# Binary cross entropy on one core: the stores of the full chunks go from the GpSimd queue to the SyncE queue

## The chip, the cores and the metric

The kernel runs on one core of a Trainium2 chip. The metric is the device time of one execution in microseconds; of several runs the median is taken. The core has five engines with instruction streams of their own. Here DVE (VectorE) and ACT (ScalarE) compute, and POOL (GpSimd), SP (SyncE) and, once, ACT issue transfers between the chip's memory (HBM) and the on-chip memory (SBUF). The transfers themselves run on 16 DMA engines, which all of these queues share.

## The reference

```
pred, target: 8192 x 8192, float32; target is 0 or 1
pred = clip(pred, 1e-7, 1 - 1e-7)
return -(target * log(pred) + (1 - target) * log(1 - pred))
```

Since a target is 0 or 1, the kernel computes -log|p + t - 1|, which is -log(p) for t = 1 and -log(1 - p) for t = 0.

## The kernel before

The arrays are taken as flat runs of elements and cut into 39 chunks. Each chunk lies over all 128 partitions: 8192 columns for chunk 0, 14336 for chunks 1 to 35, and 6656, 6656 and 1024 for the last three, called a, b and c (chunks 36 to 38). In the code z is 35, the last full chunk.

The pred values of a chunk are loaded into one of three slots of `ring_p` (slot k mod 3; a, b and c share the slot of chunk 33), are worked on in place, and are stored from there. So load_p(k+2) writes the slot of chunk k-1 and may not begin before store(k-1) has landed. The targets go to `ring_t`, one buffer of a single chunk's width, and are cast to bf16 on the way; so load_t(k+1) may not begin before both halves of merge(k) have read the old targets.

The work on a chunk is done in two halves (whole for a, b and c):

- clip (L85, DVE): the two bounds, in one instruction;
- merge (L91, DVE): p + (t - 1); then Abs (L94, ACT) and Ln (L95, ACT);
- negate (L99, DVE): times -1.

The order on each engine is that of the program, written out by hand under `manual_schedule`. Each round of the main loop (L110 to L120) issues: both merges of chunk k; load_t(k+1); both negates of k; both clips of k+1; store(k); load_p(k+2). An engine that waits holds up all that is behind it in its own stream, and no other engine.

All loads go through POOL's queue, but for load_p(0), which ACT issues. The function `store` (L75) chooses the queue of a store: POOL for chunks 0 to 35, SP for a, b and c. In POOL's stream a round is therefore load_t(k+1), store(k), load_p(k+2). The last round issues no load_p. After the loop come the loads of a, b and c, and then negate, clip and merge of the tail with the stores between them (L121 to L141). The store of the last chunk is cut into 108, 12 and 8 partitions.

Of the kernel before, what the change touches and what calls it, by code (L numbers as in the profile page):

```python
# [1 line left out]

# [4 lines left out]

EPS = 1e-7

WIDE = 14336  # L10
SLOTS = 3
TAIL = (6656, 6656, 1024)
ROWS = (108, 12, 8)


@with_exitstack
def kernel(
    ctx: ExitStack,
    tc: tile.TileContext,
    pred: bass.AP,  # L20
    target: bass.AP,
    out: bass.AP,
):
    nc = tc.nc
    fp32 = mybir.dt.float32
    low = mybir.dt.bfloat16
    Alu = mybir.AluOpType
    Act = mybir.ActivationFunctionType
    P = nc.NUM_PARTITIONS

    R, C = pred.shape
    total = R * C // P
    rest = total - sum(TAIL)
    n = rest // WIDE
    first = rest - n * WIDE
    assert 0 < first <= WIDE and n > 4 and sum(TAIL) <= WIDE
    spots = [(first, 0)]
    spots += [(WIDE, k % SLOTS * WIDE) for k in range(1, n + 1)]
    c = (n + 1) % SLOTS * WIDE
    for w in TAIL:  # L40
        spots.append((w, c))
        c += w
    n = len(spots)
    z = n - 1 - len(TAIL)
    starts = [sum(w for w, _ in spots[:k]) * P for k in range(n)]

    pool = ctx.enter_context(tc.tile_pool(name="rings", bufs=1))
    ring_p = pool.tile([P, SLOTS * WIDE], fp32, name="ring_p", tag="ring_p")
    ring_t = pool.tile([P, WIDE], low, name="ring_t", tag="ring_t")
    warm = pool.tile([1, 8], fp32, name="warm", tag="warm")  # L50

    def chunk(ap, k):
        flat = ap.rearrange("r c -> (r c)")
        w = spots[k][0]
        return flat[starts[k] : starts[k] + w * P].rearrange("(p w) -> p w", p=P)

    def cols(ring, k, part, c):
        w = spots[k][0]
        i, m = part
        return ring[:, c + i * w // m : c + (i + 1) * w // m]  # L60

    def p_of(k, part=(0, 1)):
        return cols(ring_p, k, part, spots[k][1])

    def t_of(k, part=(0, 1)):
        return cols(ring_t, k, part, spots[k][1] % WIDE)

    def load_p(k):
        queue = nc.scalar if k == 0 else nc.gpsimd
        queue.dma_start(out=p_of(k), in_=chunk(pred, k))  # L70

    def load_t(k):
        nc.gpsimd.dma_start(out=t_of(k), in_=chunk(target, k))  # L73

    def store(k):  # L75
        queue = nc.sync if k > z else nc.gpsimd
        r = 0
        for rows in ROWS if k == n - 1 else (P,):
            queue.dma_start(out=chunk(out, k)[r : r + rows, :], in_=p_of(k)[r : r + rows, :])  # L79
            r += rows  # L80
        assert r == P

    def clip(k, *part):
        p = p_of(k, *part)
        nc.vector.tensor_scalar(  # L85
            out=p, in0=p, scalar1=EPS, scalar2=1 - EPS, op0=Alu.max, op1=Alu.min
        )

    def merge(k, *part):
        p, t = p_of(k, *part), t_of(k, *part)  # L90
        nc.vector.scalar_tensor_tensor(  # L91
            out=p, in0=t, scalar=1.0, in1=p, op0=Alu.subtract, op1=Alu.add
        )
        nc.scalar.activation(out=p, in_=p, func=Act.Abs)  # L94
        nc.scalar.activation(out=p, in_=p, func=Act.Ln)  # L95

    def negate(k, *part):
        p = p_of(k, *part)
        nc.vector.tensor_scalar(out=p, in0=p, scalar1=-1.0, scalar2=None, op0=Alu.mult)  # L99

    halves = (0, 2), (1, 2)
    with tc.manual_schedule():
        load_p(0)
        load_t(0)
        load_p(1)
        nc.vector.memset(warm, 1.0)  # L106
        nc.scalar.activation(out=warm, in_=warm, func=Act.Ln)  # L107
        for h in halves:
            clip(0, h)
        for k in range(z):  # L110
            for h in halves:
                merge(k, h)
            load_t(k + 1)
            for h in halves:
                negate(k, h)
            for h in halves:
                clip(k + 1, h)
            store(k)
            if k + 2 <= z:
                load_p(k + 2)  # L120
        for h in halves:  # L121
            merge(z, h)
        a, b, c = range(z + 1, n)
        for j in a, b, c:
            load_p(j)
            load_t(j)
        negate(z, halves[0])
        clip(a)
        negate(z, halves[1])
        store(z)  # L130
        merge(a)
        clip(b)
        merge(b)
        negate(a)
        store(a)
        clip(c)
        merge(c)
        negate(b)
        store(b)
        negate(c)  # L140
        store(c)  # L141


# [1 line left out]
_INS = ['pred', 'target']  # L145
_OUTS = [((8192, 8192), 'float32')]


# [23 lines left out]
```

## Time and profile before

| what | value |
|---|---|
| median of 3 runs | 1867.39 us (1866.88 to 1868.22) |
| the profiled execution | 1868.84 us |
| its span | 1867.1 us |
| DVE busy | 1118.2 us (60%) |
| ACT busy | 901.7 us (48%) |
| POOL busy | 283.3 us (15%) |
| POOL's queue (q0) | 16272 packets, 659.56 MB, 98.5% of 16 engines |
| SP's queue (q1) | 448 packets, 7.34 MB, 0.9% |
| ACT's queue (q10) | 144 packets, 4.19 MB, 0.6% |
| full chunks: issue to landing, median | pred 44.3 us, store 31.0 us, target 35.2 us |

How the views are read. The summary cuts the span into 40 slices and gives the busy share of each in tenths; the DMA row is the mean over the 16 DMA engines, and the row of GB/s counts the bytes that land, so that a target load counts half of what it reads. The waits say who waited for whom, with the total, the number of waits and the longest. The chain goes back from the last instruction through what released each step; "issue" is time in which the engine of the chain waited for nothing that the profile shows. In a timeline a line has the start, the duration, the engine, the line of the kernel and the operation, and in brackets how long the engine was idle before and what ended that. A line of a window has the stretch and its length, the busy time of DVE, ACT and POOL with the number of instructions, the granted clock of TensorE, the DMA share and GB/s; a transfer's packet is booked where it starts, so that very short windows can show a share over 1.

### The profile page before, as it was taken

To read this page: it belongs to the slowest core of one execution; us is meant where nothing else is said; L and a number is where in the kernel's file an instruction comes from. 1 tells how busy PE (TensorE), PEld (TensorE's weight loads), DVE (VectorE), ACT (ScalarE), POOL (GpSimd) and SP (SyncE) were. 2 spreads that over 40 slices of the span, in tenths; PEclk is the share of its full clock that TensorE was granted. 3 is DMA by queue.
4 is the path that set the end of the run, shared out by engine and by line. 5 is a ranking of instruction groups with operands and counts; after the bars stand their busy time and mean duration, and the time that the engine had idled before them with its cause. 6 is when DMAs were issued, how large, how long until landed. Compare 5 with 4: busy or idle time off the path is not lost.

```text
span 1867.1 us, 695 instructions
## 1 busy us (share of the span) xinstructions
DVE 1118.2 (60%) x226; ACT 901.7 (48%) x152; POOL 283.3 (15%) x117
## 2 busy tenths in 40 slices
DVE  4675665655556555665665556655566665556664
ACT  3555444444555555444444555555544444455555
POOL 0121111111111101111111111101111111111100
DMA  9999999999999999999999999999999999999998
GB/s 331 336 373 373 364 355 359 356 355 355 354 354 359 373 373 373 370 356 362 356 354 358 354 354 356 367 373 373 373 362 360 359 354 359 354 354 354 360 366 346
DMA packets 16869, 671.14 MB, mean 359 GB/s; under 512 B 1888, under 2 KB 1888, under 8 KB 2272
## 3 DMA queue, kind: packets, MB, share of 16 engines
q0 software_dynamic: 16272, 659.56, 98.5%
q1 hardware_dynamic: 448, 7.34, 0.9%
q10 hardware_dynamic: 144, 4.19, 0.6%
q14 instruction: 5, 0.04, 0.0%
HBM read 536.87 MB, written 268.44 MB: 431 GB/s over the span
## 4 chain that ended last, share of the span: by engine, by line
DMA 67%; issue 28%; DVE 2%; ACT 2%; POOL 0%; POOLq 0%; DVEq 0%; PEldq 0%
DMA ring_t<-in_target_dram 67%; DVE ring_p L91 2%; ACT ring_p L95 1%; ACT ring_p L94 1%; DVE ring_p L99 0%; POOL out_dram L79 0%; POOL ring_p L70 0%; DVEq L167 0%; POOLq L73 0%; POOLq L79 0%; DVEq L91 0%; PEldq L167 0%
## 5 line engine op out<-in xcount | busy, mean ns | idle before, releaser
L94 ACT ACTIVATE ring_p<-ring_p 128x7168 f32<-128x7168 f32 (+3 forms) x75 | 451.6, 6021 | 943.5 <-DVE ring_p L91 943.5
L91 DVE SCALAR_TENSOR_TENSOR ring_p<-ring_t,ring_p 128x7168 f32<-128x7168 bf16 (+3 forms) x75 | 554.8, 7436 | 236.9 <-DMA ring_t<-in_target_dram 236.8
L99 DVE TENSOR_SCALAR ring_p<-ring_p 128x7168 f32<-128x7168 f32 (+3 forms) x75 | 285.0, 3801 | 475.0 <-ACT ring_p L95 475.0
L95 ACT ACTIVATE ring_p<-ring_p 128x7168 f32<-128x7168 f32 (+3 forms) x75 | 452.1, 6028 | 2.4
L85 DVE TENSOR_SCALAR ring_p<-ring_p 128x7168 f32<-128x7168 f32 (+3 forms) x75 | 281.8, 3798 | 20.1 <-DMA ring_p<-in_pred_dram 20.1
L79 POOL DMA_DIRECT2D out_dram<-ring_p x36 | 127.4, 3540 | 730.3 <-DVE ring_p L99 730.3
L73 POOL DMA_DIRECT2D ring_t<-in_target_dram x39 | 20.7, 532 | 802.9 <-DVE ring_p L91 802.1
L70 POOL DMA_DIRECT2D ring_p<-in_pred_dram x38 | 135.3, 3560 | 0.0
L107 ACT ACT_TABLE_LOAD x1 | 1.3, 1283 | 1.1 <-PEq L156 1.1
L106 DVE MEMSET warm<- 1x8 f32 x1 | 0.1, 65 | 0.8 <-PEq L156 0.8
L107 ACT ACTIVATE warm<-warm 1x8 f32<-1x8 f32 x1 | 0.2, 208 | 0.0
L156 POOL MEMSET const-float32-0.0<- 128x1 f32 x1 | 0.1, 98 | 0.2 <-issue 0.2
L156 POOL MEMSET const-bfloat16-1.0<- 128x1 bf16 x1 | 0.1, 101 | 0.0
L156 POOL MEMSET const-float32-1.0<- 128x1 f32 x1 | 0.1, 98 | 0.0
L156 POOL MEMSET const-uint8-127<- 128x1 uint8 x1 | 0.1, 98 | 0.0
## 6 DMA issues: line engine op xcount, KB each, us to landing
ring_p<-in_pred_dram POOLq DMA_DIRECT2D x35, 7168.0 KB, 44.3
out_dram<-ring_p POOLq DMA_DIRECT2D x35, 7168.0 KB, 31.0
ring_t<-in_target_dram POOLq DMA_DIRECT2D x35, 3584.0 KB, 35.2
ring_p<-in_pred_dram POOLq DMA_DIRECT2D x2, 3328.0 KB, 33.6
out_dram<-ring_p SPq DMA_DIRECT2D x2, 3328.0 KB, 15.1
ring_p<-in_pred_dram ACTq DMA_DIRECT2D x1, 4096.0 KB, 19.5
out_dram<-ring_p POOLq DMA_DIRECT2D x1, 4096.0 KB, 21.4
ring_t<-in_target_dram POOLq DMA_DIRECT2D x2, 1664.0 KB, 28.8
```

Of the source, the lines that this page charges most:

```text
L70: queue.dma_start(out=p_of(k), in_=chunk(pred, k))
L73: nc.gpsimd.dma_start(out=t_of(k), in_=chunk(target, k))
L79: queue.dma_start(out=chunk(out, k)[r : r + rows, :], in_=p_of(k)[r : r + rows, :])
L85: nc.vector.tensor_scalar(out=p, in0=p, scalar1=EPS, scalar2=1 - EPS, op0=Alu.max, op1=Alu.min)
L91: nc.vector.scalar_tensor_tensor(out=p, in0=t, scalar=1.0, in1=p, op0=Alu.subtract, op1=Alu.add)
L94: nc.scalar.activation(out=p, in_=p, func=Act.Abs)
L95: nc.scalar.activation(out=p, in_=p, func=Act.Ln)
L99: nc.vector.tensor_scalar(out=p, in0=p, scalar1=-1.0, scalar2=None, op0=Alu.mult)
L106: nc.vector.memset(warm, 1.0)
L107: nc.scalar.activation(out=warm, in_=warm, func=Act.Ln)
L156: nc = _bacc.Bacc("TRN2", target_bir_lowering=False, num_devices=1)
```

## The change

One line of `store` chooses another queue. The stores of chunks 0 to 34 are issued by SP instead of POOL, as those of a, b and c are already. The store of chunk 35 stays on POOL, behind the loads of the tail. POOL's stream in a round is then load_t(k+1), load_p(k+2), and SP's is store(k). What each transfer depends on is unchanged: a store waits for its negate, and a load of pred for the store that frees its slot.

```diff
     def store(k):
-        queue = nc.sync if k > z else nc.gpsimd
+        queue = nc.gpsimd if k == z else nc.sync
         r = 0
         for rows in ROWS if k == n - 1 else (P,):
             queue.dma_start(out=chunk(out, k)[r : r + rows, :], in_=p_of(k)[r : r + rows, :])
```

## The prediction

> **What bounds the kernel now.** I read the summary of the span first, then the waits, the chain, one period of the timeline, and last short windows at the beginning and the end.
>
> ```profile
> DMA  9999999999999999999999999999999999999998
> ...
> HBM read 536.87 MB, written 268.44 MB: 431 GB/s over the span
> ```
>
> The 16 DMA engines are busy from end to end, while DVE stands at 60% and ACT at 48%. All 805 MB go through them, so time can be won or lost only where the engines run dry or where a row of data costs more.
>
> ```profile
> POOL ring_t L73 <- DVE ring_p L91: 802.1, 37, 31.3
> POOL out_dram L79 <- DVE ring_p L99: 730.3, 36, 20.6
> ...
> DVE ring_p L91 <- DMA ring_t<-in_target_dram: 236.8, 35, 7.7
> ```
>
> The third line is the compute side's only wait for data in the steady state: merge (L91) waits 6.9 us per chunk for its target. The first two are POOL's, which has time to spare. No wait of POOL for an old store is listed: load_p never has to wait for a free slot.
>
> ```profile
> 1017.97 15.49 issue
> 1033.46 0.01 POOLq L79
> 1033.48 35.20 DMA ring_t<-in_target_dram
> ```
>
> The chain repeats two pieces: 15.49 us, in which both halves of merge read the one target buffer, and 35.20 us from the issue of the next target load to its landing. Together 50.7 us, the period.
>
> ```profile
> 932.00 0.53 POOL L73 DMA_DIRECT2D ring_t<-in_target_dram  x1 [22.16 <-DVE ring_p L91]
> ...
> 948.89 3.89 DVE L99 TENSOR_SCALAR ring_p<-ring_p 128x7168 f32<-128x7168 f32 x1 [8.38 <-ACT ring_p L95]
> 952.70 7.70 DVE L85 TENSOR_SCALAR ring_p<-ring_p 128x7168 f32<-128x7168 f32 x2
> 953.08 3.63 POOL L79 DMA_DIRECT2D out_dram<-ring_p  x1 [20.55 <-DVE ring_p L99]
> 956.70 3.82 POOL L70 DMA_DIRECT2D ring_p<-in_pred_dram  x1
> 967.28 15.16 DVE L91 SCALAR_TENSOR_TENSOR ring_p<-ring_t,ring_p 128x7168 f32<-128x7168 bf16 x2 [6.88 <-DMA ring_t<-in_target_dram]
> ...
> 982.74 0.53 POOL L73 DMA_DIRECT2D ring_t<-in_target_dram  x1 [22.22 <-DVE ring_p L91]
> ```
>
> ```profile
> 982.00:1032.74 50.74, 30.56 (x7) 24.60 (x5) 7.96 (x3) 1.00 1.00 362
> ```
>
> Call the issue of load_t(k+1) time 0 of chunk k. Its store is issued at 21, compute would be ready for the next merge at 28.4 (953 + 7.4), and the target lands at 35.2. The window over one period has a DMA share of 1.00. In it each engine moves 24 rows: the queue table has 144 packets for one transfer, which are 128 rows and 16 small ones, so 8 rows per engine and transfer, and three transfers per chunk. A row takes 50.74/24 = 2.114 us, a transfer 16.9. Since 35.2 is far over 16.9, the target spends 18.3 us behind older transfers: the queue orders it, not the buffer alone. Without queueing the loop would take 28.4 + 15.5 = 43.9 us, so compute has 6.8 us of slack per chunk.
>
> **What it removes.** 35 store issues leave POOL (about 3.62 us each; the other entries of that line's 127.4 us are short). They lie inside POOL's 730 us of waiting and shift nothing that DMA lacks: just before the store takes effect, 10.6 us of load_t are still queued (35.2 less 24.6). Worth 0; without that cover it would be worth at most 3.6 us a chunk.
>
> **What it moves.** The store goes to SP, which holds nothing else until the tail's three stores, and is issued at 20.8 instead of 24.6. SP's first store in the tail, issued at 1838.73, starts its first row 2.6 us later by the packet records, so I let the store begin at 23.4. It is now no longer behind load_t(k+1) in one queue but beside it. How two queues share an engine is seen in the first stretch, where load_p(0) (ACT's queue) and load_t(0) (POOL's) overlap, in windows of one row's time:
>
> ```profile
> 4.80:6.00 1.20, 0.00 (x0) 0.00 (x0) 0.00 (x0) 1.00 1.01 437
> 6.00:7.20 1.20, 0.00 (x0) 0.00 (x0) 0.00 (x0) 1.00 1.02 218
> 7.20:8.40 1.20, 0.00 (x0) 0.00 (x0) 0.00 (x0) 1.00 1.02 437
> 8.40:9.60 1.20, 0.00 (x0) 0.00 (x0) 0.00 (x0) 1.00 1.02 218
> 9.60:10.80 1.20, 0.00 (x0) 0.00 (x0) 0.00 (x0) 1.00 1.02 437
> ```
>
> 437 GB/s is a window of f32 rows, 218 one of target rows (bf16 lands half the bytes): strict alternation, one row each. So from 23.4 until load_t's last row, every second row is the store's. The period stays 50.7 as long as DMA is never dry, so the latency of load_t must stay 35.2; of its wait, 10.3 to 11.8 us (23.4 to 33.7 or 35.2, by how long a landing lags its last row) are then shared half and half. That is 5.2 to 5.9 us of rows newer than load_t; I take 5.5. For the same latency, 5.5 us less of older rows may be ahead of it: every merge stands 5.5 us later against the bytes moved than before. In the steady state this costs nothing. At the end, where no loads are left to fill DMA, it does. Before, the end belongs to compute already:
>
> ```profile
> 1850.00:1852.00 2.00, 0.99 (x2) 0.00 (x0) 0.00 (x0) 1.00 0.75 320
> ```
>
> DMA drops to 0.75 when the last wide negate ends and store(b) can go. From merge(35) on, the ACT and DVE steps fix the distance to that store, so the 5.5 us reach the end whole: **+5.5** (rows come whole, so 4.2 to 8.5).
>
> **What it adds.** load_p(k+2) now follows load_t(k+1) at once on POOL, and waits there for store(k-1), which shares its time with loads and lands about 4 to 8 us after time 0 (issued at -30, 34 us at half rate, and landing). Behind it on POOL is load_t(k+2), due only at 50.7. POOL's queue holds 24 us of rows then, so no row is late. Its descriptor time, 3.82 when it meets clips, is covered by the same 24. Cost 0; above that cover, each us late costs up to 35 us in all.
>
> Switching queues row by row: in the packet records of the alternating stretch, an f32 row and a target row together take 2.43 us, 1.215 each, against 1.2075 for equal rows alone. 8 ns a row, at 16 alternating rows less the 3 changes of transfer that a period has already, over 35 chunks: **+3.4**. Reads of SBUF between reads of HBM are not shown; the bounds are 0 and twice that on this reading, and worse or better are rivals. I take the measured pair.
>
> **The beginning.** load_p(2) has a free slot, and now goes at 34 instead of after store(0) at 49.7. That fills the one dry spot before:
>
> ```profile
> 52.00:54.00 2.00, 1.43 (x1) 0.00 (x0) 1.55 (x1) 1.00 1.45 215
> 54.00:56.00 2.00, 0.00 (x0) 0.00 (x0) 0.00 (x0) 1.00 0.09 14
> ```
>
> Windows book a row where it starts: 16 rows started near 53 took 3.1 us instead of 2.1. **-1.0**.
>
> **The tail.** load_p(a) no longer follows store(34), and lands before DVE asks for it (0.76 us of wait go, but ACT's Ln at 1811.96 ends later anyway: 0). load_t(b) lands earlier against compute: merge(b) waited 1.65 us, of which the ACT gap of 0.75 before Abs(b) matters: **-0.65**. Less of store(a) is left when store(b) starts, 0.8 us before, 0 to 0.8 gained: **-0.4**.
>
> **Sum.** 5.5 + 3.4 - 1.0 - 0.65 - 0.4 = +6.85. The profiled execution took 1868.84 us (span 1867.1), 1.45 above the median of the runs, 1867.39. On the median: **1874.2**.
>
> **Rivals.** *Served transfer by transfer* (1866.4): if an engine finished all eight rows of load_t before it turned to the store, the order of rows would be the old one, the lag and the row switching both 0, and only the -1.0 stays. Against it: the alternating windows; for it: those are two queues of loads, no store among them. The Trainium skill, "DMA: Bandwidth & Descriptors", section "Queues, rings and completion order", says an engine drains a whole packet, typically 9 to 17 descriptors, from a queue before switching; eight rows and a semaphore write are nine, so by that rule this rival is the outcome. The trace disagrees with that reading: 437 and 218 alternate every 1.2 us.
>
> *Faster: reads of two kinds overlap.* If SBUF rows and HBM rows, alternating on an engine, hide part of each other, every alternating row gets cheaper. It beats the lag from 13 ns a row on (7.2 us over 560 rows gives 1863.65, where faster begins); 25 ns would give 1867.4 + 3.45 - 14 = 1857. For it: shares of 1.02 in the mixed windows, above 1.00. Against: the pair there took 2.43, not less than two rows.
>
> *Alternating store and load rows cost more than two loads do*: each 10 ns a row is 5.6 us; 25 ns gives 1867.4 + 3.45 + 14 = 1885. No window of before shows it either way.
>
> *Stores starve*: if SP's rows got much less than half, store(k-1) would hold back load_p, POOL's queue would empty 34 us after time 0, and DMA would idle. Store landing would have to take 64 us instead of 34 to 38; from there each us is 35 in all: 1890 and up. The half-and-half windows speak against it.
>
> **How the numbers follow.** A run of this kernel can tell about 0.2%, 3.7 us: slower is above 1871.1, faster below 1863.65. Forecast 0.50; its own range is 1869.1 (4.2 and no row cost, 0.8 gained) to 1881 (8.5 and 6.8), of which 0.08 lies under 1871.1. Transfer by transfer 0.14 (same). Overlap 0.16 (faster). Dearer rows 0.13, starving 0.07 (slower). So faster 0.16, same 0.22, slower 0.62. The range reaches to the other cases, 1861 to 1886; it leaves out the stronger half of the overlap (0.09), the dearest rows (0.05) and most of starving (0.05).
>
> **What would show it.** In the profile after: stores on the hardware queue q1, some 260 MB; POOL's wait of load_p for out_dram, a few us each, and none of DVE for pred; the period still 50.7 to 50.9; load_t still near 35; issue times of load_t some 5 us further into the bytes moved, merge(35) about 8 us later than 1779.6; DMA share below 1 for longer just before the last stores; no gap at 54. If load_t lands in much under 35 us while DMA is at 1.00, or a row costs other than 2.11 to 2.13, I am wrong.

## The result and the profile after

The changed kernel takes 1923.68 us (median of 4 runs, 1916.02 to 1937.93) against 1867.81 for the kernel before: a ratio of 1.031, 95% interval 1.028 to 1.034. The forecast was 1874.2 with a range up to 1886. The sign was right, the size was not. The profiled execution is the slowest of the four (1937.93 us, span 1936.2).

The page of the changed kernel, DMA row, bytes and the issues of the full chunks (count, KB each, median us from issue to landing):

```profile
DMA  9999999989999998999999999999999899999998
...
HBM read 536.87 MB, written 268.44 MB: 416 GB/s over the span
...
ring_p<-in_pred_dram POOLq DMA_DIRECT2D x35, 7168.0 KB, 52.8
out_dram<-ring_p SPq DMA_DIRECT2D x34, 7168.0 KB, 38.6
ring_t<-in_target_dram POOLq DMA_DIRECT2D x35, 3584.0 KB, 32.5
```

DMA now has slices below 0.9, and the same bytes move at 416 instead of 431 GB/s. The target's median latency is even shorter than before. It is the spread that matters, and the waits show it (total us, times, longest):

```profile
POOL ring_p L70 <- DMA out_dram<-ring_p: 310.6, 22, 23.9
DVE ring_p L91 <- DMA ring_t<-in_target_dram: 304.9, 25, 27.7
```

The first line is new: load_p waits for an old store, 22 times and up to 23.9 us. Merge waited about 6.9 us for its target in nearly every chunk before; now it waits up to 27.7 in some chunks and not at all in others. Five issues in POOL's stream and one merge, from the timeline, show a bad stretch:

```profile
331.81 0.53 POOL L73 DMA_DIRECT2D ring_t<-in_target_dram  x1 [40.56 <-DVE ring_p L91]
356.29 3.33 POOL L70 DMA_DIRECT2D ring_p<-in_pred_dram  x1 [23.95 <-DMA out_dram<-ring_p]
391.04 15.16 DVE L91 SCALAR_TENSOR_TENSOR ring_p<-ring_t,ring_p 128x7168 f32<-128x7168 bf16 x2 [27.73 <-DMA ring_t<-in_target_dram]
406.49 0.53 POOL L73 DMA_DIRECT2D ring_t<-in_target_dram  x1 [46.88 <-DVE ring_p L91]
407.01 0.53 POOL L70 DMA_DIRECT2D ring_p<-in_pred_dram  x1
450.25 0.53 POOL L73 DMA_DIRECT2D ring_t<-in_target_dram  x1 [42.71 <-DVE ring_p L91]
```

Target loads were 50.7 us apart before. Here they are 74.7 us apart, and then 43.8. That second figure is the loop without any queueing, the 28.4 + 15.5 of the prediction. The target issued at 331.81 is there for merge only at 391, some 59 us later. Over the whole run the distances swing between 43.8 and 75. Three windows of the same run:

```profile
1003.50:1028.90 25.40, 19.61 (x4) 9.99 (x2) 0.53 (x1) 1.00 1.00 432
102.00:136.00 34.00, 23.65 (x5) 21.68 (x4) 0.53 (x1) 1.00 1.02 388
398.00:406.00 8.00, 8.00 (x2) 7.27 (x2) 0.00 (x0) 1.00 0.36 158
```

In the first, pred rows and store rows alternate at full speed. In the second they alternate as well, the DMA engines are never idle, and yet only 388 GB/s move: by the packet records the pred rows take 2.57 us on average, the store rows 2.26. In the third most of the DMA engines have nothing to do.

So there are two losses. From the packet records come, as means over the 16 DMA engines and in us, the time without any packet (dry; the last 12 us or so, in which only the last stores run, are left out) and the time by which rows lasted longer than usual, which is 2.116 us (f32) and 2.131 us (targets) in the full chunks; the shorter rows of the other chunks are held against their own usual time:

```
kernel    span     over before   dry    longer rows   both, over before
before    1867.1                 0.9     3.7
after     1936.2     +69.1      28.7    46.3          +70.4
```

The two account for the whole difference. They are not fully separate: the last row before a dry spot lasts longer too (3.1 us at 53 in the kernel before), and in the bad stretch above pred rows of 2.4 to 2.9 us between 315 and 350 come before the late target and the dry spot at 400.

### The profile page after: what moved, and what is told of

Its sections match the earlier page's. It is cut to its first block, busy times and chain, and to the rows that moved or that the text cites. A ratio compares the mean times of both kernels' runs of the same rounds, so it can differ in the third digit from the quotient of the medians.

```text
span 1936.2 us, 733 instructions
## 1 busy us (share of the span) xinstructions
DVE 1117.3 (58%) x226; ACT 901.6 (47%) x152; POOL 62.5 (3%) x82
## 4 chain that ended last, share of the span: by engine, by line
DMA 44%; DVE 28%; ACT 19%; another core or an unknown queue 5%; issue 3%; DVEq 0%; POOLq 0%
DMA ring_t<-in_target_dram 43%; DVE ring_p L91 21%; ACT ring_p L95 10%; ACT ring_p L94 9%; DVE ring_p L85 5%; DVE ring_p L99 3%; DMA ring_p<-in_pred_dram 1%; DVEq L167 0%; DVEq L91 0%; POOLq L73 0%; POOLq L70 0%
## 5 line engine op out<-in xcount | busy, mean ns | idle before, releaser
L70 POOL DMA_DIRECT2D ring_p<-in_pred_dram x38 | 41.2, 1083 | 311.2 <-DMA out_dram<-ring_p 310.6
L79 POOL DMA_DIRECT2D out_dram<-ring_p x1 | 0.5, 541 | 19.5 <-DVE ring_p L99 19.5
## 6 DMA issues: line engine op xcount, KB each, us to landing
out_dram<-ring_p SPq DMA_DIRECT2D x34, 7168.0 KB, 38.6
```

## The experiments

**Is it the swing, or is it rows that alternate?** First the changed kernel with more DVE work, so that no chunk can run early:

```diff
             for h in halves:
                 clip(k + 1, h)
+            for h in (0, 2), (2, 4):
+                clip(k + 1, h)
```

> The changed kernel with 5.84 us more of DVE work per chunk: after the two clips of a chunk, one and a half of its halves are clipped once more (which changes no value). The earliest next merge moves from 43.8 us after the issue of a target load to about 49.6, so a chunk can hardly run early against the DMA engines' 50.7. Theory SWING (the two queues let the period swing between 43.8 and 60 to 75, and the long chunks leave DMA dry and make it restart): the swing goes, issues of target loads are 50 to 52 us apart, and the time falls, although work was added, to 1868 to 1885. Theory ROWS (rows of stores and loads that alternate on an engine cost more by themselves, 41 of the 69 us): the period becomes even but the rows stay slow, 1905 to 1915. If neither matters and added work only adds: 1925 or more.

1908.89 us, ratio 1.023 (1.021 to 1.025). Added work made it about 15 us faster, and the target loads come evenly:

```profile
600.53 0.53 POOL L73 DMA_DIRECT2D ring_t<-in_target_dram  x1 [42.38 <-DVE ring_p L91]
...
652.21 0.53 POOL L73 DMA_DIRECT2D ring_t<-in_target_dram  x1 [42.67 <-DVE ring_p L91]
...
703.89 0.53 POOL L73 DMA_DIRECT2D ring_t<-in_target_dram  x1 [43.04 <-DVE ring_p L91]
```

They are 51.7 us apart; after the first eight chunks the distances stay between 50.8 and 53.0. Dry time falls from 28.7 to 6.6 us, while the longer rows stay at 40.6. The swing costs the dry time; the slow rows are another matter, and with them the time comes out where ROWS had it (1905 to 1915).

Then the kernel before with one single store on SP:

```diff
-        queue = nc.sync if k > z else nc.gpsimd
+        queue = nc.sync if k > z or k == 17 else nc.gpsimd
```

> The kernel before with a single store, that of chunk 17, on SP; all others on POOL's queue. SWING: the target load issued before that store lands up to 8 us late, the next ones are back to 35.2 within two chunks because one queue pulls them back, and the total is within 3 us of before. ROWS: some 16 alternating rows per engine cost about 1.2 us (41/35), total within 3 us too, but the rows of that stretch are longer than 2.116 us by 0.07 on average. If one disturbance is enough to keep the period swinging, issues stay uneven to the end and the time is 10 us or more above before.

1875.82 us in one run, with before at 1866.94: one store costs nearly 9 us, three times what either theory allowed. The issues of target loads around it, the landing of the disturbed target (from the chain), the next store, and one window:

```profile
881.39 0.53 POOL L73 DMA_DIRECT2D ring_t<-in_target_dram  x1 [22.59 <-DVE ring_p L91]
...
942.90 0.53 POOL L73 DMA_DIRECT2D ring_t<-in_target_dram  x1 [59.33 <-DVE ring_p L91]
...
963.99 3.62 POOL L79 DMA_DIRECT2D out_dram<-ring_p  x1 [20.56 <-DVE ring_p L99]
...
986.66 0.53 POOL L73 DMA_DIRECT2D ring_t<-in_target_dram  x1 [15.24 <-DVE ring_p L91]
...
1037.21 0.53 POOL L73 DMA_DIRECT2D ring_t<-in_target_dram  x1 [22.03 <-DVE ring_p L91]
```

```profile
881.39 45.96 DMA ring_t<-in_target_dram
```

```profile
960.00:970.00 10.00, 10.00 (x3) 0.00 (x0) 6.01 (x2) 1.00 0.51 155
```

The distances are 61.5, 43.8 and 50.6: one disturbance, one early chunk, and the single queue is back in step. The disturbed target landed 46.0 us after its issue instead of 35.2. By the packet records the store's rows began at 905.65; the target would have needed 10.9 us more, and at half rate that takes twice as long. Being 10.8 us late uses up the 10.6 us that POOL's queue held in reserve by the prediction. The next store, issued at 963.99, starts its first row 4.0 us after that, so DMA ran dry for 4.4 us around 962 to 968.

**Do alternating rows cost anything by themselves?** All transfers without the arithmetic, with the stores out of a fixed slot, in two queues and in one:

```diff
+        for k in range(n):
+            nc.gpsimd.dma_start(out=t_of(k), in_=chunk(target, k))
+            nc.sync.dma_start(out=chunk(out, k), in_=slot(k, 2))    # nc.gpsimd in the other
+            nc.gpsimd.dma_start(out=slot(k, k % 2), in_=chunk(pred, k))
```

> Transfers alone: all target and pred loads of the kernel before from POOL, and all stores from SP, the stores out of a slot that is filled once and never written again. Clip, merge, Abs, Ln and negate are left out, so nothing waits for compute and the stores run beside the loads from the start. SWING: rows cost the same in one queue or two; the time is within 8 us of the same transfers in one queue. ROWS: at least 30 us more than in one queue, since as many rows alternate as in the changed kernel.

> The same transfers alone, all from POOL in the order target load, store, pred load. Clip, merge, Abs, Ln and negate are left out. Both theories: DMA saturated from end to end, 805 MB at 434 GB/s, 1855 to 1868 us. It is the base for the two-queue stream.

Two queues 1874.52 us, one queue 1882.06. The base came out higher than expected, in part because in one queue everything behind the first store waits while DVE fills the slot (12.0 us): that costs it some 4 us of DMA time in the first 50 us, so these two times alone show no gain of the second queue. But two queues are not the slower ones, and in the packet records rows alternate at about 433 GB/s (HBM bytes) for 1200 us, until the stores are done; over the whole run the rows of the full chunks are 3 us longer than usual. Alternating as such is nearly free, so the theory ROWS fell in that form. What was left was the alignment: in the changed kernel, when the pred rows beside a store are sorted by how many rows load k+2 was ahead of store k, the excess stands out at one place:

```
rows ahead         -4    -3    -2    -1     0     1     2     3
excess, ns/row      9     8    18   138   416   174    36    64
```

In the two-queue stream the lag was never between -2 and 4. I therefore took pred loads and stores alone:

```diff
+        for k in range(1, z - 1):
+            nc.sync.dma_start(out=chunk(out, k), in_=slot(2))
+            nc.gpsimd.dma_start(out=slot((k + 1) % 2), in_=chunk(pred, k + 2))
```

> Half of the transfers alone: 33 stores of full chunks from SP out of one fixed slot, beside 33 pred loads from POOL, the load of chunk k+2 starting with the store of chunk k, so that both queues are at the same row of their chunks (lag 0). All target loads, all arithmetic, chunks 0 and 35 to 38 of the output and the first pred loads are left out. Without any loss 66 transfers of 16.91 us: 1116 us and 3 at the ends. Theory SAME-ROW (rows of a store and a pred load at the same place of their chunks hinder each other, 0.42 us a row at lag 0 in the changed kernel): 1116 plus 30 to 110 us, 1150 to 1230. Theory COMPUTE (rows are only slow beside DVE and ACT): 1119 to 1130.

> The same half of the transfers, but SP first stores the upper half of the partitions' rows of chunk 35 once, so that each later store trails its load by four rows per engine (lag 4); left out is what the lag 0 stream leaves out. SAME-ROW: 66.5 transfers without slow rows, 1125 to 1135. COMPUTE: the same as lag 0 plus 8.

1150.02 and 1153.28 us, of which the fill of the slot is the first 16. Neither had the lag that it was built for: POOL's first load began some 5 us (in the second 9 us) after SP's first store. By the packet records the loads were up to 2.9 rows behind in the one and about 3 ahead in the other. Both ran without slow rows, at 434 GB/s; this is the first:

```profile
60.00:1100.00 1040.00, 0.00 (x0) 15.90 (x30) 1.00 1.00 434
```

So they show that pred loads and stores can take turns at full speed, and nothing on lag 0. Two tries to change the places instead:

> The lag 0 stream with the rows of each stored chunk put to other places of the same chunk in HBM (partition 8a+b goes to row 16b+a), while the SBUF side is as it was; the output has permuted rows, and what lag 0 leaves out is left out. If SAME-ROW comes from the SBUF side (the same partition read and written at once): as slow as lag 0. If it comes from the places in HBM: no slow rows or other ones, 1119 to 1135.

1213.02 us with the stored rows permuted, at 380 to 430 GB/s. This permutation changes the order of the places in HBM and may also change which engine gets which row, so it tells no more than that one other pairing of rows is slower. In the paced kernel, the stores cut in two:

```diff
+        if k < z:
+            for r in P // 2, 0:
+                queue.dma_start(out=chunk(out, k)[r : r + P // 2, :], in_=p_of(k)[r : r + P // 2, :])
+            return
```

> The paced kernel (5.84 us of repeated clips per chunk, stores from SP; 1908.9 us), its stores before chunk 35 cut into two of 64 partitions, the upper half first, so that the store's rows are half a chunk away from those of the pred load beside it. SAME-ROW: the slow rows (39 us of row time over nominal in the paced kernel) go for the greater part, 1870 to 1885. COMPUTE, or two queues by themselves: no change beyond 5 us, 1904 to 1915.

2124.43 us, 215 us more than the paced kernel. The remedy was worse than the loss, and the two further runs below tell why. First a scan: the stream of pred loads and stores, with one extra row per engine from SP before every fourth store (of chunks 5, 9, 13 and so on), so that the lag moves through the whole chunk.

```diff
+            if k % 4 == 1 and k > 1:
+                nc.sync.dma_start(out=chunk(out, z)[k // 4 * 16 - 16 : k // 4 * 16, :], in_=slot(2)[:16, :])
```

> 33 stores of full chunks from SP out of one fixed slot beside 33 pred loads from POOL (chunk k+2 with chunk k), all else left out; before every fifth store SP writes one extra row per engine, so that the lag between load and store grows by one row every four chunks, from about -2.5 to +4.5, through 0. Theory SAME-ROW: in the third and fourth stretch of four chunks (about 290 to 560 us) the rate falls from 434 to 380 to 400 GB/s, as between 100 and 140 us in the changed kernel, and elsewhere it is 434; in all 1150 to 1180. Theory COMPUTE (rows are slow only beside the arithmetic of DVE and ACT): 434 everywhere, 1150 or less.

1225.62 us. Windows of four stretches with steady lags:

```profile
640.00:720.00 80.00, 0.00 (x0) 1.58 (x3) 1.00 1.00 433
770.00:850.00 80.00, 0.00 (x0) 1.05 (x2) 1.00 1.00 434
900.00:1030.00 130.00, 0.00 (x0) 1.58 (x3) 1.00 0.98 360
1080.00:1160.00 80.00, 0.00 (x0) 1.06 (x2) 1.00 1.00 431
```

With no arithmetic at all, one stretch of 130 us runs at 360 GB/s with the DMA engines busy: COMPUTE falls. There the load is 8.5 rows ahead, half a row ahead of the place where the next chunk's load and store are level; that fits the table above. But in the first passage near level rows (190 to 260 us, the load less than one row behind) 434 GB/s moved. Level rows alone do not decide it. The scan again, with the stores further on in HBM by 64 rows, and by 3:

> The same scan with every store going half a chunk further in HBM (64 rows of 57344 bytes), its SBUF side unchanged; all else is left out as in the scan. If SAME-ROW holds by the SBUF side: the slow stretch is where it was in the scan. If it holds by the places in HBM: the slow stretch is gone or is elsewhere. COMPUTE: 434 everywhere in both.

> The scan of lags with every store going 3 rows (172032 bytes) further in HBM, the SBUF side unchanged; all else is left out as in the scan. If slow rows come from the places in HBM, the sustained slow stretch (355 GB/s from 865 to 1060 us in both scans) moves by three lags, to other stretches of four chunks, or goes. If they come from the SBUF side or from the order of rows alone, it stays at 865 to 1060 us with 350 to 365 GB/s.

1231.47 and 1226.35 us. The same window, with 64 rows and then with 3:

```profile
900.00:1030.00 130.00, 0.00 (x0) 1.59 (x3) 1.00 0.96 353
900.00:1030.00 130.00, 0.00 (x0) 1.59 (x3) 1.00 0.97 359
```

The slow stretch stays where it was, so for these two shifts at least the places in HBM are not what decides. And the paced kernel with all transfers cut in two, once in the same order, once with the stores' halves exchanged:

> The paced kernel with every transfer of chunks 1 to 34, and the loads of 35, cut into two of 64 partitions, lower half first, loads and stores alike. Theory ENGINE-MATCH (a row is slow where the engine that stores from a group of partitions is another than the one that loads into it; cutting the stores alone broke the match and cost 215 us): back to the paced kernel's 1909, within 25 us. If cutting by itself costs the time: 2080 to 2150 as with the stores alone cut.

> As e12, but the stores' upper half first, so that a store and a load that start together are never at the same partitions. SAME-ROW on the SBUF side with matched engines: 15 to 35 us less than e12. If only the match of engines counts, or the place in the chunk does not matter: within 10 us of e12.

2474.96 and 2493.96 us. Both are far above what ENGINE-MATCH had, and above the 2080 to 2150 for cutting by itself; the exchange brought nothing. One window of the first, in which by the packet records only the halves of a pred load are under way:

```profile
82.00:112.00 30.00, 19.06 (x3) 19.46 (x4) 2.06 (x4) 1.00 1.03 214
```

A transfer to 64 partitions moves 214 GB/s with all 16 engines busy, half of the 434 to 128. The Trainium skill, "SBUF — State Buffer", section "Door 1: The DMA port swizzle (why `[64,N]` ≈ `[32,N]`)", has it so: partitions 0 to 63 reach 8 of 16 ports, at 27.2 GB/s each, which makes 218. The trace agrees. It explains why cutting was so dear. It also means that the three runs with cut transfers say nothing on the match of engines or on level rows, since the loss by cutting covers both. Whether the slow rows too are a matter of which partitions are read and written at once, no run here shows.

**Without pred loads beside stores.** The decisive run puts the pred loads of the full chunks into SP's queue behind the stores, where the two never take turns:

```diff
-        queue = nc.scalar if k == 0 else nc.gpsimd
+        queue = nc.scalar if k == 0 else nc.sync if k <= z else nc.gpsimd
```

> The changed kernel with the pred loads of chunks 1 to 35 on SP too, behind the stores; POOL's queue holds the target loads (and the tail). Stores and pred loads no longer take turns on an engine, targets take turns with both. If the slow rows come from stores and pred loads side by side: row time over nominal falls from 41 us to under 12. The time depends on the target's latency too: at half the rows it lands 34 to 38 us after its issue, a period of 50.7 to 53.5, 1868 to 1955 us. If any two queues side by side give slow rows: 30 us or more of row time over nominal.

1889.56 us, ratio 1.012 (1.011 to 1.014). The longer rows are down to 10.1 us. Of the rest, 14 lie in one place:

```profile
38.00:52.00 14.00, 13.16 (x4) 4.80 (x2) 0.22 (x1) 1.00 0.00 0
```

Chunk 1's load on SP had shared the engines with chunk 0's, so that the first compute started at 38.31 instead of 20.21 and nothing was left to move. With `1 < k <= z` in place of `k <= z` that load is on POOL again:

> As e14, but the pred load of chunk 1 on POOL behind the targets of chunk 0, as in both original kernels; SP has the pred loads of chunks 2 to 35 and the stores. If the dry start made 14 of the 22 us: 1870 to 1878. If the second queue costs the time in the steady state: 1883 to 1890.

1872.31 us, ratio 1.002 (1.001 to 1.003). In the middle of the run it keeps step as the kernel before did, with two queues:

```profile
736.02 0.53 POOL L73 DMA_DIRECT2D ring_t<-in_target_dram  x1 [50.24 <-DVE ring_p L91]
786.80 0.53 POOL L73 DMA_DIRECT2D ring_t<-in_target_dram  x1 [50.26 <-DVE ring_p L91]
837.58 0.53 POOL L73 DMA_DIRECT2D ring_t<-in_target_dram  x1 [50.25 <-DVE ring_p L91]
```

The books of all of them, as for the first two:

```
kernel                        span    over before   dry   longer rows   both, over before
after                        1936.2     +69.1      28.7    46.3          +70.4
after, paced                 1908.5     +41.4       6.6    40.6          +42.6
before, one store on SP      1874.1      +7.0       4.9     6.3           +6.6
pred loads on SP             1887.3     +20.2      14.9    10.1          +20.4
pred loads from 2 on SP      1869.9      +2.8       2.0     6.6           +4.0
```

No version beat the kernel before; there DMA is dry for 0.9 us and rows are 3.7 us longer than usual in all, so that there is little left to win on this side.

## Why the prediction was wrong

- **What bounds the kernel** was right: DMA. All of the loss is dry engines and dearer rows.
- **Two queues share an engine row by row**: right for the order. One engine's rows in the changed kernel, in the records (kind, start, us; S a store): p1002.4 2.12, S1004.5 2.12, p1006.6 2.12, S1008.7 2.12. The rival in which whole transfers are served one by one was wrong. It took each row for one of the 9 to 17 descriptors of a packet. The Trainium skill, "DMA: Bandwidth & Descriptors", section "Queues, rings and completion order", has an engine drain a whole packet from a queue before it switches. The trace agrees with that as far as each packet of the records is one row; how many descriptors a row is, the records do not show.
- **"The period stays 50.7 as long as DMA is never dry ... In the steady state this costs nothing" (+5.5)** is the first step that failed. I asked what a steady state would look like and not whether it is reached. The single store shows the first overtaking: the target is 10.8 us late, not 5.5, because all that it still lacked goes at half rate, and only 10.6 us were in reserve. (The store's first row also starts later than the prediction read off the tail: 3.5 us after the issue there and in the single-store run, not 2.6.) With the stores of the other full chunks in POOL's queue, one early chunk follows and then the kernel is in step again. In the changed kernel the next store disturbs the next target, and late and early chunks follow one another to the end. That is the dry time, 27.8 us over before: it goes for the greater part when the paced kernel takes the early chunks away. The lag itself can't be read off there; where the two queues do keep step (pred loads from 2 on SP) the whole cost is 4.8 us.
- **"POOL's queue holds 24 us of rows then, so no row is late. Cost 0"** failed with it. Stores took 38.6 us in the median and up to 43.6 instead of 34, load_p waited for them up to 23.9 us, and the queue that I had counted on was not there. Starving, which got 0.07 and was to begin with stores that take 64 us, happens well under that.
- **Row switching (+3.4)** was the other large miss: the longer rows made 42.6 us over before. The pair of rows that I measured at the start of the run was one of two loads, with no store in it. The two-queue stream and the first two windows of the scan show that loads and stores too can take turns at next to no cost, but only in some alignments; I took one pair for all. That a store and a pred load side by side cause the slow rows is shown by the run that separates them (10.1 us instead of 46.3); that it depends on how they stand to one another, by the scan; that their place in HBM does not decide, by its two shifts. What makes it so stays open. The rival of dearer rows (0.13) was thus a good part of the truth: 42.6 us over its 560 rows is 76 ns a row, against the 25 of its example.
- **The beginning (-1.0)** did not come: target rows around 47 to 52 us last longer in the changed kernel as well (up to 3.4 us), as the first store begins. **The tail (-0.65, -0.4)** is below what these runs can tell.
- The sentence of the Trainium skill that issuing from several engines only saves the issuing time ("DMA: Bandwidth & Descriptors", section "Issuing engines are not separate DMA queues") holds for the bytes: the two-queue stream is no slower than one queue. It does not hold for this kernel's time, +3.1%, since here the second queue changes the order of arrival, and with it who waits, and which rows run side by side.

## What to carry to other kernels

In this kernel one queue in which all transfers stand in the order of need is a regulator: a chunk that comes early queues longer, and the pipeline falls back into step, as after the single store. Before you move transfers to another queue, ask which transfer they will overtake, by how much it can then be late at half rate, and whether the queue holds more reserve than that; a calculated steady state is not enough. If a second queue is wanted, put the transfers that hinder one another, here the stores and the loads into the same ring, into the same queue.

## What the runs showed of the hardware that was not expected

- Loads and stores that take turns on the DMA engines run at 434 GB/s in one alignment and at 353 to 360 in another, with all engines busy and no arithmetic beside them.
- Loads to 64 partitions run at 214 GB/s instead of 434 (4.40 us a row instead of 2.12), and cutting all transfers of the paced kernel so cost 566 us (2474.96 against 1908.89).
- The 16 DMA engines drift apart: by the packet records their last rows of a target load end about 4 us apart in the median before, 7 in the changed kernel, 12 in the stream of two queues, but also about 10 in the stream of one, so it is not the second queue alone. A load has landed only with the last of them: the last row of the target issued at 932.00 in the kernel before ends at 966.9, and the target has landed at 967.2.
- More work can be faster: 5.84 us of useless clipping per chunk took about 15 us off the changed kernel.
